# A decoder layer on one core: GpSimd's elementwise work in the router stage moved to VectorE and ScalarE, rank products a tile later

## The chip, the cores and the metric

One core of one Trainium2 chip runs the kernel. Its engines are TensorE (PE in the profile, with PEld for the loads of the stationary operand), VectorE (DVE), ScalarE (ACT), GpSimd (POOL) and SyncE (SP, which issues most DMAs). The metric is the device time of one execution in microseconds (us).

## The reference, cut to what matters

One decoder layer over 512 tokens of width 1024, all in float32. After two attention branches, a gated sum goes through `w_out`; the result is normalised, and a router picks one of four groups and two of its eight experts for every token:

```python
mixed = sigmoid(g_sb) * (o_sb @ w_sb) + sigmoid(g_mla) * (o_mla @ w_mla)
x  = layer_norm(ALPHA * x + gate1 * (mixed @ w_out), ln1_g, ln1_b)
u2 = x * (1 + scale2) + shift2
g_idx   = top_1(softmax(u2 @ w_rg + b_rg))                 # of 4 groups
top_idx = top_2((u2 @ w_re + b_re) of that group)          # of 8 experts
moe = sum over the two experts of weight * (silu(u2 @ w_g) * (u2 @ w_u)) @ w_d
x  = layer_norm(ALPHA * x + gate2 * moe, ln2_g, ln2_b)
```

## The kernel before, in words

**Order of the work.** The program is traced once and a planner orders each engine's queue by its own estimate of times, with program order as the priority; each engine then executes its queue strictly in order. Inside a `manual_schedule` block the named engines keep the order in which the block was written; two such blocks can still be interleaved with one another.

**The stages around the change.** (1) Both attentions run until about 397 us. (2) The MLA branch product: for each of eight blocks m of 128 columns, PE multiplies the branch weights (split into a high and a low part, `whi` by ScalarE L681, `wlo` by VectorE L682) with the attention output, three matmuls for each of four k. `evac_mix` then gates the result (L717, VectorE), adds the other branch's part (L718, GpSimd), casts to `mixh` (L719, ScalarE) and subtracts to `mixl` (L722, VectorE). (3) The product with `w_out`, again three matmuls for each of eight k, tile t of 128 tokens and column half nh. `split_wo(nh, kh)` makes the high and low parts of four k: it multiplies the loaded rows by `gate1` (L799, GpSimd and VectorE in turn), casts (L800, ScalarE) and subtracts (L801, VectorE). The split (1, 1) writes the buffer `RB`, which (0, 1) held. The half nh = 0 runs for all four tiles at once into four PSUM banks `o`; `evac_o` adds the residual x (L810) and takes statistics (L811), both on VectorE. In the middle of that half the norm's gain and bias are loaded into `lng1` and scaled by ALPHA (L887, GpSimd).

(4) **The tile loop.** The half nh = 1 runs tile by tile into PSUM banks `oh` (two buffers). Between its matmuls the loop places the routing of the tile before: `route_half` transposes the unnormalised row block (L971), copies it (`vT`, L973 VectorE and L974 ScalarE) and multiplies it by the router weights (`pl`, L976); `norm1` turns the statistics into scale and shift; `norm1_out` writes the normalised rows to the DRAM tensor `xhd` (cast L941 on ScalarE, DMA from GpSimd's queue L943), and for tiles 0 and 1 also the affine result (two GpSimd operations over 128x1024, L947) to `xnd` (L948). `route` is a chain of small VectorE operations from the logits (L980) by two maxima with their indices and a cast (L989) to the one-hot rows `A` (L991) and their sum `Ab` (L992), followed at once by the **rank products** on PE (L994), which count for each token how many tokens before it chose the same expert.

(5) After the loop, a chain of small VectorE operations goes from the counts (L1023, L1027) to the gather indices `gidx` (L1055). Other short chains are traced behind it: the table of expert slots (L1071 to L1092), the softmax weights (`combine_weights`, L1146 to L1154), the overflow list (L1174 to L1177). (6) GpSimd's queue gathers rows of `xhd` by `gidx` (L1133), which are transposed (L954), made affine (L960, L958) and fed to the experts.

**Weights of the experts.** They come in pieces of 1 MB into a ring of 15 buffers, each of which is a buffer of the earlier stages first (`W1` held `lng1`, `B0` and `B1` the rows x); SP issues a load as soon as the buffer is free, in the order of its queue.

Of the kernel before, what the change touches and what calls it, by code (L numbers as in the profile page):

```python
# [17 lines left out]
ALU = mybir.AluOpType  # L18
# [34 lines left out]
def tile_layer(ctx: ExitStack, tc: tile.TileContext, x, c, positions, w_ada, b_ada, w_in, mla_q_norm_g, w_q_up,  # L53
# [661 lines left out]
    def evac_mix(a, m):  # L715
        g0, g1 = part(gat, m), part(gat, 8 + m)
        DVE.tensor_tensor(g1, a, g1, ALU.mult)  # L717
        POOL.tensor_tensor(g0, g0, g1, ALU.add)  # L718
        ACT.copy(part(mixh, m), g0)  # L719
        for n in range(2):  # L720
            lo = slice(n * 2 * P, (n + 1) * 2 * P)
            DVE.tensor_tensor(mixl[n][:, m, :], g0[:, lo], part(mixh, m)[:, lo].bitcast(F32), ALU.subtract)  # L722
# [67 lines left out]
    def split_wo(nh, kh):  # L790
        t = raws["wo", nh, kh]
        tags = wtag[nh, kh]
        if len(tags) == 1:
            w8 = gran(tags[0], [KD, 512], F32R, "wo")
            hi, lo = w8[:, 0:4, :], w8[:, 4:8, :]
        else:
            hi, lo = (gran(g, [4, 512], F32R, "wo") for g in tags)
        for k in range(4):
            (POOL if k % 2 else DVE).tensor_tensor(t[:, k, :], t[:, k, :], gate1[:, nh * 512:(nh + 1) * 512], ALU.mult)  # L799
            ACT.copy(hi[:, k, :], t[:, k, :])  # L800
            DVE.tensor_tensor(lo[:, k, :], t[:, k, :], hi[:, k, :].bitcast(F32), ALU.subtract)  # L801
        wo[nh, kh] = (hi, lo)
# [5 lines left out]
    def evac_o(a, t, nh):  # L808
        xs = xr[t // 2][:, t % 2, nh * 512:(nh + 1) * 512]
        DVE.scalar_tensor_tensor(xs, xs, ALPHA, a, ALU.mult, ALU.add)  # L810
        DVE.bn_stats(stats[t][:, nh, :], xs)  # L811
# [66 lines left out]
    for k in range(KD):  # L878
        if k == 4:
            split_wo(1, 0)  # L880
            lng1 = gran("W1", [2, D], F32, "lng1")
            load_wo(1, 1)()
            for i in range(2, 6):
                load_gran(i)
            for n, v in enumerate((ln1_g, ln1_b)):
                SP.dma_start(lng1[:, n], v[0].partition_broadcast(P))
            POOL.tensor_scalar(lng1, lng1, ALPHA, None, ALU.mult)  # L887
            router_consts()
        for t in range(NT):
            mm_o(a4[t], t, k, 0, k == 0, k == KD - 1)  # L890
# [46 lines left out]
    def norm1_out(t):  # L937
# [6 lines left out]
        if t < 2:  # L944
            ACT.activation(r, r, AF.Identity, bias=m[:, 3:4], scale=m[:, 2:3])
            for n, op in ((0, ALU.mult), (1, ALU.add)):
                POOL.tensor_tensor(r, r, lng1[:, n], op)  # L947
            POOL.dma_start(xnd[t * P:(t + 1) * P, :], r)  # L948
# [29 lines left out]
    def route(t):  # L978
# [13 lines left out]
        DVE.tensor_tensor(Ab[:, t, :], A[:, t, 0, :], A[:, t, 1, :], ALU.add)  # L992
        for t2 in range(t + 1):
            PE.matmul(prk[:, t * 32:t * 32 + 32], triu if t2 == t else onesb, Ab[:, t2, :], start=(t2 == 0), stop=(t2 == t))  # L994

    for t in range(NT):
        a = pt("fil", 2, "oh")
        for k in range(KD):
            mm_o(a, t, k, 1, k == 0, k == KD - 1)
            if k == 1 and t > 0:  # L1000
# [3 lines left out]
            if k == 4:  # L1004
                route_half(t, 0)
        evac_o(a, t, 1)
# [9 lines left out]
    with tc.manual_schedule(engines={mybir.EngineType.Pool}):  # L1016
        norm1_out(NT - 1)
        POOL.memset(gran_tile(13)[0:1, 0:1], 0.0)
    route(NT - 1)
    for i in range(10, 14):  # L1020
        load_gran(i)
    for t in range(NT):
        PE.matmul(prk[:, 128:160], onesb, Ab[:, t, :], start=(t == 0), stop=(t == NT - 1))  # L1023

    with tc.manual_schedule(engines={mybir.EngineType.DVE}):
# [29 lines left out]
        DVE.tensor_tensor(gidx, gif[:, 0, :], gif[:, 1, :], ALU.add)  # L1055
# [14 lines left out]
    with tc.manual_schedule(engines={mybir.EngineType.DVE}):  # L1070
# [95 lines left out]
    DVE.tensor_scalar(pq[:, 0:1], pcol, -2.0, float(CAP - 1), ALU.mult, ALU.add)  # L1166
    DVE.memset(pq[:, 1:2], 1.0)
# [164 lines left out]
    with tc.manual_schedule(engines=MS):  # L1332
        start = tc.manual_schedule(engines={mybir.EngineType.DVE, mybir.EngineType.Activation})
        start.__enter__()
        combine_weights()
# [45 lines left out]
        for n, u in enumerate(units):  # L1381
# [42 lines left out]
            if n == 1:  # L1424
                y_rows()
                overflow_list()
# [229 lines left out]
```

## Time and profile before

| | |
|---|---|
| median of three runs | 825.21 us (820.85 to 825.68) |
| the profiled execution | 827.33 us, of which the span from the first to the last instruction is 825.6 us |
| PE busy | 691.5 us (84%) |
| VectorE busy | 524.3 us (64%) |
| ScalarE busy | 249.7 us (30%) |
| GpSimd busy | 217.8 us (26%) |
| mean granted clock of PE | 0.929 of 2.4 GHz |
| moved by DMA | 195.15 MB |

A busy share is a mean over stages of different kinds; the stage of the change lies between about 397 and 525 us of the span. Clock 1.00 is 2.4 GHz, and 0.50 is 1.2 GHz; a value between is a mean over a stretch with both.

### The profile page before, as it was taken

The page shows a single profiled execution, that of the slowest core. Times are in us where ns is not written, and L with a number is a line of the kernel's source. Part 1 is how long each engine was busy: PE and PEld are TensorE (multiplying, and loading weights), DVE is VectorE, ACT ScalarE, POOL GpSimd, SP SyncE. Part 2 cuts the span into 40 slices and gives each one's busy share as a digit, 9 for nine tenths or more (in the row PEclk, how much of TensorE's full clock was granted, in tenths as well). Part 3 has the DMA queues.
Part 4 walks back from the last instruction along what each step waited for, and adds up shares of the span by engine and source line. Part 5 has one row for each costly group of instructions (what it writes and reads, how often), then busy time and mean ns, then how long its engine had stood idle before and what let it go on. Part 6 is the DMA issues. An engine that isn't in the chain of part 4 may idle for free. (4 is left out here: it accounts for less than half of the span.)

```text
span 825.6 us, 10607 instructions
## 1 busy us (share of the span) xinstructions
PE 691.5 (84%) x3201; PEld 426.7 (52%) x3201; DVE 524.3 (64%) x1083; ACT 249.7 (30%) x545; POOL 217.8 (26%) x269
## 2 busy tenths in 40 slices
PE   5789999999999798999989665777889779977880
PEld 3568877677776464666668553432333223322330
DVE  3995366867746857876596766664834715543297
ACT  2123244333435434443231324342201101111411
POOL 5546022322333312200363440300000000028174
PEclk9999999999999898999999867698999889999995
DMA  9964365547612793331549348788999998899942
GB/s 266 257 178 129 111 223 197 191 153 249 207 32 66 272 363 120 89 124 54 202 180 359 124 144 286 247 292 293 389 410 417 400 415 325 298 357 402 349 183 102
DMA packets 92109, 195.15 MB, mean 236 GB/s; under 512 B 11421, under 2 KB 53498, under 8 KB 86154
## 3 DMA queue, kind: packets, MB, share of 16 engines
q1 hardware_dynamic: 88544, 182.71, 62.5%
q0 software_dynamic: 3424, 11.57, 4.0%
q8 instruction: 36, 0.59, 0.3%
q14 instruction: 31, 0.25, 0.1%
q10 hardware_dynamic: 74, 0.03, 0.0%
HBM read 173.30 MB, written 35.67 MB: 253 GB/s over the span
## 5 line engine op out<-in xcount | busy, mean ns | idle before, releaser
L1224 PE MATMUL pgu<-ex,xT 128*64 128x512 f32 (+1 forms) x608 | 119.5, 615 | 17.7 <-DMA ex<-in_w_exp_up_dram 10.6
L1224 PEld LDWEIGHTS pgu<-ex,xT 128*64 128x64 f32 (+1 forms) x608 | 49.1, 129 | 82.3 <-issue 71.1
L330 PE MATMUL acc<-uh,whi 128*128 128x512 f32 x224 | 90.9, 406 | 0.0
L330 PE MATMUL acc<-uh,wlo 128*128 128x512 f32 x224 | 88.3, 394 | 0.4 <-DVE wlo L321 0.4
L330 PE MATMUL acc<-ul,whi 128*128 128x512 f32 x224 | 87.6, 391 | 0.0
L1254 PE MATMUL py<-ex,hT 128*64 128x512 f32 (+1 forms) x304 | 66.2, 668 | 17.7 <-DVE hT L1247 12.8
L577 POOL TENSOR_TENSOR w<-be,sc 128x128 f32<-128x128 f32 (+3 forms) x32 | 39.6, 1239 | 135.6 <-DVE sc L575 113.0
L1232 ACT ACTIVATE sl<-pgu 128x256 f32<-128x256 f32 x33 | 11.4, 383 | 173.7 <-PE pgu L1224 154.3
L1294 POOL DMA_DIRECT2D lraw<-in_ln_g_dram x4 | 2.0, 510 | 203.2 <-DVE lraw L1291 203.2
L330 PEld LDWEIGHTS acc<-uh,whi 128*128 128x128 f32 x224 | 42.1, 188 | 14.6 <-issue 4.4
L321 DVE TENSOR_TENSOR wlo<-raw,whi 128x1024 fp32r<-128x1024 f32 x27 | 34.4, 1272 | 21.8 <-ACT whi L320 21.6
L330 PEld LDWEIGHTS acc<-uh,wlo 128*128 128x128 f32 x224 | 42.0, 188 | 11.2 <-DVE wlo L321 2.0
L1254 PEld LDWEIGHTS py<-ex,hT 128*64 128x64 f32 (+1 forms) x304 | 16.9, 135 | 59.2 <-issue 29.2
L443 DVE SCALAR_TENSOR_TENSOR macc<-ra,rtx,macc 128x1024 f32<-128x1024 f32 x28 | 38.4, 1394 | 13.5 <-DMA ra<-in_w_ada_dram 13.4
L330 PEld LDWEIGHTS acc<-ul,whi 128*128 128x128 f32 x224 | 42.2, 188 | 7.9 <-issue 0.2
L1233 DVE TENSOR_TENSOR sl<-pgu,sl 128x256 f32<-128x256 f32 x33 | 12.9, 419 | 43.3 <-ACT sl L1232 43.3
L320 ACT CAST whi<-raw 128x1024 fp32r<-128x1024 f32 x27 | 28.4, 1051 | 29.5 <-PE acc L330 14.2
L1247 DVE COPY hT<-phT 128x256 f32<-128x256 f32 x33 | 13.2, 419 | 32.6 <-PE phT L1239 19.7
L575 DVE TENSOR_TENSOR_SCAN sc<-al 128x127 f32<-128x127 f32 (+3 forms) x32 | 27.1, 849 | 10.5 <-ACT al L571 8.6
L817 PE MATMUL oh<-wo,mixh 128*128 128x512 f32 x64 | 28.7, 497 | 5.8 <-DVE wo L801 5.8
L536 PE MATMUL px<-ident,w 128*128 128x128 f32 x160 | 28.9, 280 | 5.3 <-POOL w L577 2.1
L1217 DVE COPY xT<-XRA 128x128 f32 (+1 forms) x30 | 7.6, 252 | 34.7 <-PE pgu L1224 29.7
(491 smaller groups left out, 1515.5 us busy)
## 6 DMA issues: line engine op xcount, KB each, us to landing
ex<-in_w_exp_gate_dram SPq DMA_DIRECT2D x64, 512.0 KB
ex<-in_w_exp_up_dram SPq DMA_DIRECT2D x64, 512.0 KB
ex<-in_w_exp_down_dram SPq DMA_DIRECT2D x32, 1024.0 KB
ra<-in_w_ada_dram SPq DMA_DIRECT2D x16, 1024.0 KB
raw<-in_w_in_dram SPq DMA_DIRECT2D x12, 1024.0 KB
Ys<-dq SPq DMA_DIRECT2D x10, 1024.0 KB
ada<-in_w_ada_dram SPq DMA_DIRECT2D x16, 512.0 KB
rwo<-in_w_out_dram SPq DMA_DIRECT2D x6, 1024.0 KB
```

What stands on the lines that cost most here:

```text
L320: ACT.copy(hi, w)
L321: DVE.tensor_tensor(lo, w, hi.bitcast(F32), ALU.subtract)
L330: PE.matmul(a, w_[:, k, :], part(u_, k), start=(k == 0 and n == 0), stop=(k == nk - 1 and n == 2))
L443: DVE.scalar_tensor_tensor(o, v, cact[:, k, 0:1], o, ALU.mult, ALU.add)
L536: PE.transpose(px[:, kt * P:(kt + 1) * P], w[:, kt * P:(kt + 1) * P], ident)
L575: DVE.tensor_tensor_scan(sc[:, 0:W - 1][:, ::-1], al[:, 1:W][:, ::-1], al[:, 1:W][:, ::-1], 1.0, ALU.mult, ALU.bypass)
L577: POOL.tensor_tensor(w[:, 0:W], be[:, 0:W], sc[:, 0:W], ALU.mult)
L817: PE.matmul(a, u_, w_[:, k % 4, :], start=first and n == 0, stop=last and n == 2)
L1224: PE.matmul(ps_t[rows, :], xT[u, t][:, k, rows], ew[e, k // 4][:, :, k % 4, :], start=(k == 0), stop=(k == KD - 1))
L1233: DVE.tensor_tensor(sl, ps_t[:, DE:2 * DE], sl, ALU.mult)
L1247: DVE.tensor_copy(hT[u, min(t, 1)][:, t // 2], phT[:, o:o + 256].rearrange("p (k n) -> p k n", k=2))
L1254: PE.matmul(pys[nh][rows, :], hT[u, min(t, 1)][:, t // 2, k, rows], ew[e, 2][:, k, nh * 512:(nh + 1) * 512], start=(k == 0), stop=(k == 1))
```

## The change

`evac_mix`: the add goes to VectorE. `split_wo`: no multiply by `gate1` for the first column half, all four on VectorE for the second; instead `evac_o` multiplies the first half's PSUM result in place. `lng1` is scaled on ScalarE. The affine of tiles 0 and 1 leaves `norm1_out`, goes to VectorE and is called two tiles later, as are the rank products; the products of the counts are issued for three tiles before the last tile's routing. The first four k of tiles 0 and 1 of the second half run ahead of the loop. The short chains that aren't part of the way to `gidx` are queued behind it on VectorE.

```diff
@@ evac_mix
         DVE.tensor_tensor(g1, a, g1, ALU.mult)
-        POOL.tensor_tensor(g0, g0, g1, ALU.add)
+        DVE.tensor_tensor(g0, g0, g1, ALU.add)
         ACT.copy(part(mixh, m), g0)
@@ split_wo
         for k in range(4):
-            (POOL if k % 2 else DVE).tensor_tensor(t[:, k, :], t[:, k, :], gate1[:, nh * 512:(nh + 1) * 512], ALU.mult)
+            if nh:
+                DVE.tensor_tensor(t[:, k, :], t[:, k, :], gate1[:, 512:1024], ALU.mult)
             ACT.copy(hi[:, k, :], t[:, k, :])
@@ evac_o
+        if nh == 0:
+            DVE.tensor_tensor(a, a, gate1[:, 0:512], ALU.mult)
         DVE.scalar_tensor_tensor(xs, xs, ALPHA, a, ALU.mult, ALU.add)
@@ first half, k == 4
-            POOL.tensor_scalar(lng1, lng1, ALPHA, None, ALU.mult)
+            ACT.activation(lng1, lng1, AF.Copy, scale=ALPHA)
@@ norm1_out
         if t < 2:
             ACT.activation(r, r, AF.Identity, bias=m[:, 3:4], scale=m[:, 2:3])
-            for n, op in ((0, ALU.mult), (1, ALU.add)):
-                POOL.tensor_tensor(r, r, lng1[:, n], op)
-            POOL.dma_start(xnd[t * P:(t + 1) * P, :], r)
+
+    def norm1_affine(t):
+        r = xr[t // 2][:, t % 2, :]
+        for n, op in ((0, ALU.mult), (1, ALU.add)):
+            DVE.tensor_tensor(r, r, lng1[:, n], op)
+        POOL.dma_start(xnd[t * P:(t + 1) * P, :], r)
@@ route and the tile loop
         DVE.tensor_tensor(Ab[:, t, :], A[:, t, 0, :], A[:, t, 1, :], ALU.add)
+
+    def rank(t):
         for t2 in range(t + 1):
             PE.matmul(prk[:, t * 32:t * 32 + 32], triu if t2 == t else onesb, Ab[:, t2, :], start=(t2 == 0), stop=(t2 == t))
+    ah = {t: pt("fil", 2, "oh") for t in range(2)}
+    for t in range(2):
+        for k in range(4):
+            mm_o(ah[t], t, k, 1, k == 0, False)
     for t in range(NT):
-        a = pt("fil", 2, "oh")
-        for k in range(KD):
+        a = ah[t] if t < 2 else pt("fil", 2, "oh")
+        for k in range(4 if t < 2 else 0, KD):
             mm_o(a, t, k, 1, k == 0, k == KD - 1)
-            if k == 1 and t > 0:
+            if k == (5 if t < 2 else 1) and t > 0:
                 route_half(t - 1, 1)
                 norm1_out(t - 1)
                 route(t - 1)
             if k == 4:
                 route_half(t, 0)
+            if k == 5 and t > 1:
+                rank(t - 2)
+                norm1_affine(t - 2)
@@ after the loop
+    def count(*ts):
+        for t in ts:
+            PE.matmul(prk[:, 128:160], onesb, Ab[:, t, :], start=(t == 0), stop=(t == NT - 1))
+
+    rank(NT - 2)
+    count(0, 1, 2)
     route(NT - 1)
     for i in range(10, 14):
         load_gran(i)
-    for t in range(NT):
-        PE.matmul(prk[:, 128:160], onesb, Ab[:, t, :], start=(t == 0), stop=(t == NT - 1))
+    count(3)
+    rank(NT - 1)
@@ the index chain and what follows it
-        DVE.tensor_tensor(gidx, gif[:, 0, :], gif[:, 1, :], ALU.add)
+        gidx_at = DVE.tensor_tensor(gidx, gif[:, 0, :], gif[:, 1, :], ALU.add).ins
-    with tc.manual_schedule(engines={mybir.EngineType.DVE}):
+    with tc.issue_after(gidx_at), tc.manual_schedule(engines={mybir.EngineType.DVE}):
...
+    with tc.issue_after(gidx_at):
+        DVE.tensor_scalar(pq[:, 0:1], pcol, -2.0, float(CAP - 1), ALU.mult, ALU.add)
+        DVE.memset(pq[:, 1:2], 1.0)
...
-        combine_weights()
+        with tc.issue_after(gidx_at):
+            combine_weights()
...
-                overflow_list()
+                with tc.issue_after(gidx_at):
+                    overflow_list()
```

`issue_after(i)` queues what its block traces on the engine of instruction `i` behind `i`.

## Rows read from the trace of the kernel before

**Rows 1.** The page, part 1 (busy us of an engine, share of the span, instructions) and one group of part 5 (line, engine, operation, output and inputs, count, busy us and mean ns of one, idle time before).

```profile
PE 691.5 (84%) x3201; PEld 426.7 (52%) x3201; DVE 524.3 (64%) x1083; ACT 249.7 (30%) x545; POOL 217.8 (26%) x269
...
L321 DVE TENSOR_TENSOR wlo<-raw,whi 128x1024 fp32r<-128x1024 f32 x27 | 34.4, 1272 | 21.8 <-ACT whi L320 21.6
```

**Rows 2.** The table by stage: from and to in us, length, then busy us and instructions of PE, PEld, VectorE, ScalarE and GpSimd, the granted clock, the DMA engines' share and GB/s.

```profile
397.00:417.00 20.00, 17.41 (x72) 12.47 (x71) 13.80 (x29) 6.32 (x11) 8.20 (x6) 1.00 0.58 196
417.00:430.00 13.00, 9.95 (x35) 7.23 (x35) 13.00 (x15) 4.14 (x7) 9.20 (x6) 0.87 0.24 85
430.00:450.00 20.00, 20.00 (x106) 17.16 (x105) 12.20 (x14) 4.57 (x8) 8.53 (x6) 1.00 0.90 341
450.00:462.00 12.00, 6.20 (x26) 4.67 (x25) 12.00 (x17) 2.18 (x4) 5.58 (x2) 0.86 0.55 220
462.00:475.00 13.00, 12.22 (x61) 9.93 (x61) 7.00 (x22) 6.09 (x7) 3.38 (x3) 0.86 0.36 121
475.00:490.00 15.00, 10.49 (x47) 8.38 (x47) 10.59 (x23) 4.49 (x5) 6.93 (x5) 0.75 0.38 141
490.00:505.00 15.00, 12.82 (x63) 9.95 (x62) 7.89 (x27) 3.30 (x4) 2.71 (x5) 0.79 0.64 200
505.00:515.00 10.00, 1.44 (x14) 1.17 (x13) 8.41 (x54) 5.98 (x8) 0.61 (x2) 0.58 0.98 367
```

**Rows 3.** PE's waits between 397 and 515 us: who waited for what, us in total, times, longest.

```profile
PE prk L994 <- DVE Ab L992: 10.0, 3, 3.4
PE oh L817 <- DVE wo L801: 5.8, 1, 5.8
...
PE o L817 <- DVE wo L801: 1.6, 1, 1.6
PE o L817 <- ACT wo L800: 1.4, 1, 1.4
```

**Rows 4.** PE in order of time: start us, us, engine, line, operation, output and input, shape, count of merged instructions.

```profile
430.15 0.62 PE L817 MATMUL o<-wo,mixh 128*128 128x512 f32 x2
...
430.84 0.62 PE L817 MATMUL o<-wo,mixh 128*128 128x512 f32 x2
...
461.74 1.05 PE L817 MATMUL oh<-wo,mixh 128*128 128x512 f32 x2
...
463.02 1.05 PE L817 MATMUL oh<-wo,mixh 128*128 128x512 f32 x2
...
467.19 0.60 PE L971 MATMUL pu<-ident,xr_B 128*128 128x128 f32 x4
...
467.86 0.39 PE L817 MATMUL oh<-wo,mixl_R 128*128 128x512 f32 x1
...
468.32 0.62 PE L976 MATMUL pl<-rtx,vT 128*128 128x40 f32 x4
...
469.10 0.39 PE L817 MATMUL oh<-wo,mixl_R 128*128 128x512 f32 x1
```

**Rows 5.** VectorE in order of time, the tile loop.

```profile
457.26 4.78 DVE L801 TENSOR_TENSOR wo<-rwo,wo 128x512 fp32r<-128x512 f32 x4
...
472.81 1.93 DVE L989 CAST ixf<-ix 128x2 f32<-128x2 uint32 x1
474.78 2.54 DVE L991 TENSOR_SCALAR A<-iot,ixf 128x32 f32<-128x32 f32 x2
...
498.63 0.26 DVE L980 SCALAR_TENSOR_TENSOR Lg<-pl,mv,msk_mla 128x40 f32<-128x40 f32 x1 [0.90 <-PE pl L976]
...
500.81 0.16 DVE L989 CAST ixf<-ix 128x2 f32<-128x2 uint32 x1
501.01 0.39 DVE L991 TENSOR_SCALAR A<-iot,ixf 128x32 f32<-128x32 f32 x2
```

**Rows 6.** GpSimd in order of time, the same stretch.

```profile
456.05 5.37 POOL L887 TENSOR_SCALAR lng<-lng 128x2048 f32<-128x2048 f32 x1 [5.84 <-DMA lng<-in_ln_b_dram]
...
472.35 4.79 POOL L947 TENSOR_TENSOR xr_B<-xr_B,lng 128x1024 f32<-128x1024 f32 x2 [0.29 <-DVE Lg L986]
```

**Rows 7.** Three lines of the kernel: count, then min/median/max ns of one, first and last start in us.

```profile
L717 DVE TENSOR_TENSOR gat<-acc,gat x8: 677/682/691, 398.7 to 426.5; 128x512 f32<-128x512 f32 x8
...
L718 POOL TENSOR_TENSOR gat<-gat,gat x8: 1295/1666/1670, 399.4 to 427.2; 128x512 f32<-128x512 f32 x8
...
L817 PE MATMUL oh<-wo,mixh x64: 388/476/797, 450.3 to 503.2; 128*128 128x512 f32 x64
```

**Rows 8.** VectorE in order of time, behind the tile loop: the count, the gather indices and the first affine of gathered rows.

```profile
510.48 0.19 DVE L1027 COPY cnt<-prk 128x32 f32<-128x32 f32 x1
...
516.64 0.16 DVE L1055 TENSOR_TENSOR gidx<-gif 128x8 int32<-128x8 f32 x1
...
522.85 1.37 DVE L960 TENSOR_SCALAR XRA<-pxg,vc 128x128 f32<-128x128 f32 x4 [3.95 <-PE pxg L954]
```

**Rows 9.** GpSimd in order of time: issues of the first and third gather.

```profile
517.09 1.12 POOL L1133 DMA_INDIRECT xg<-xhd,gidx  x1 [7.42 <-DVE gate L1175]
...
519.83 0.99 POOL L1133 DMA_INDIRECT xg<-xhd,gidx  x1 [0.30 <-issue]
```

**Rows 10.** SP's waits between 395 and 520 us, in the same form as rows 3.

```profile
SPq L865 <- POOL xr_B L947: 15.9, 1, 15.9
```

**Rows 11.** The table by stage for a stretch of the expert stage, in the form of rows 2.

```profile
600.00:620.00 20.00, 18.02 (x84) 7.25 (x86) 5.12 (x11) 0.77 (x2) 0.00 (x0) 1.00 1.02 414
```

More of the change, by code (lines that the diff above doesn't have):

```diff
@@ L1165, in tile_layer @@
     pq = posf[:, 0, :]
-    DVE.tensor_scalar(pq[:, 0:1], pcol, -2.0, float(CAP - 1), ALU.mult, ALU.add)
-    DVE.memset(pq[:, 1:2], 1.0)
+    with tc.issue_after(gidx_at):
+        DVE.tensor_scalar(pq[:, 0:1], pcol, -2.0, float(CAP - 1), ALU.mult, ALU.add)
+        DVE.memset(pq[:, 1:2], 1.0)
     ovt = gate1[:, 0:5 * 32 * TOV].rearrange("p (a e k) -> p a e k", a=5, e=32)
```

## The prediction

> **What bounds the kernel now.** I read the page first: PE is busy for 84% of the span [rows 1]. Busy time doesn't say at which clock, so the second view is the table by stage [rows 2]. Before 397 us nothing is edited, and from 525 us on the expert stage runs. Between them lies the router stage, and there PE is neither idle for good nor full: from 450 to 505 us it is busy 41.7 of 55 us at a granted clock of 0.75 to 0.86, while from 430 to 450 us it is busy all the time at 1.00. The third view is PE's own waits [rows 3]: three waits of about 3.4 us for `Ab` (L992) in front of the rank products (L994), two of them in the tile loop and one at its end; 5.8 us for the second split of `w_out` (L801); 1.6 and 1.4 us for its first split. None of these is a wait for a transfer. The fourth view is PE in order of time [rows 4]: three matmuls of 512 columns follow one another in 0.69 us at 2.4 GHz (430.15 to 430.84), and in 1.28 us right behind the stall that ended at 460.3 (461.74 to 463.02), which is the level of 1.2 GHz. So every stall is paid twice: once as idle time, once as slow matmuls after it.
>
> Why VectorE is late is in its rows beside GpSimd's [rows 5, 6]. In the first tile the two compares of L991 (128x32) take 2.54 us and the cast before them 1.93; in the third tile the same take 0.39 and 0.16. The slow pair lies inside GpSimd's two 128x1024 operations of L947 (472.35 to 477.1), the fast one beside nothing on GpSimd. The four subtractions of L801 take 4.78 us from 457.26, while GpSimd scales `lng1` (456.05 to 461.4). So what bounds the stage is one chain, PE to VectorE to PE, whose VectorE part is stretched by GpSimd's elementwise work.
>
> **The change part by part.**
>
> *MLA product loop, `evac_mix` (397 to 420 us).* Eight adds leave GpSimd, 1.67 us each, and become VectorE adds; the nearest row is the multiply of the same shape in front of them, 0.68 [rows 7]. ScalarE's cast to `mixh` waits for that add, and the cast for a later weight split stands behind it in ScalarE's queue, so the add is on PE's loop. PE idles 2.6 us in 397 to 417 [rows 2]. VectorE gets 8 x 0.68 = 5.4 us in a stage where it is busy 13.8 of 20. I take back 2.0 of the 2.6 us; bounds 0.6 and 2.6.
>
> *First split of `w_out` (417 to 430 us).* The first half loses its multiplies (four on VectorE, four on GpSimd), so ScalarE casts straight from the loaded rows. PE's waits of 1.4 and 1.6 us go, and the matmuls at the slow clock after them, some 3.7 us at 1.28 instead of 0.69 per three, cost 3.7 x (1 - 0.69/1.28) = 1.7 us. Together 4.7 us; I take 4.4, lower bound 2. The loads of the next rows, which start when a `raw` buffer is free, come earlier too.
>
> *First gate in PSUM.* `evac_o` gets four multiplies of 128x512 from PSUM; 0.68 each by the row of L717 [rows 7], 2.7 us, on VectorE between the two column halves. They delay the second split L801 behind them, because that split writes the buffer which the first half has just finished reading. Twelve evacuation operations of about 0.65 us are 7.8 us, begun some 1.4 us before the first half ends; the first L801 is then ready 7 us after that end. PE now has both first tiles' first four k to run, 24 matmuls x 0.23 = 5.5 us, where it had 12. A wait of about 1.5 us is left of 5.8.
>
> *`lng1` scaled on ScalarE.* 2048 columns once. Hidden: ScalarE is busy 2.2 of 12 us in 450 to 462 [rows 2]. If its queue puts it ahead of the casts of the second split and the load is late, those casts and PE wait with it, up to the 5.4 us that the same step took on GpSimd [rows 6].
>
> *The tile loop (450.3 to 503.7 us, 53.4 us [rows 7]).* Rank products move to a tile later: they no longer stand in PE's queue in front of the next matmuls, so the two stalls of 3.4 us go, with or without GpSimd. The affine of tiles 0 and 1 goes to VectorE, four operations of 128x1024; the nearest row of two SBUF inputs, L321, has 1.27 [rows 1], 5.1 us. I count both engines again from the end of the first half. PE: 96 matmuls x 0.23 = 21.8; seven half tiles of transposes and logits, which add 0.44 (467.19 to 467.86 less one matmul) and 0.55 (468.32 to 469.10 less one) [rows 4], are 6.9; ranks 0.7; the wait above 1.5: 31 us. VectorE: 7.8 + 4 x 0.65 for L801 = 10.4; for each of three tiles 1.4 for the two halves of the residual step, 1.0 for the small norm steps, 0.8 for copies and 3.0 for the routing chain (498.63 to 501.6 [rows 5]), 18.6; affine 5.1; less the 1.4 us that it starts earlier: 32.7 us. Two queues that are both nearly full and wait for one another do not reach the larger of the sums; I add 3 us. That makes 35.5, a gain of 17.9. Bounds: PE alone without that wait, 29.5 (gain 23.9), and with the waits of the first rival below some 47 (gain 7).
>
> *The chain after the loop (503.7 to 516.8 us).* From the count (510.48) to the gather indices (516.64) VectorE takes 6.3 us [rows 8], and works on other chains between the steps of this one. The eighteen steps' own durations and their hand-overs sum to about 5.4 us; the rest, 0.9, comes back when the others stand behind `gidx`, and the earlier count products give 0.1: gain 1.0, bounds 0 and 1.5.
>
> *What now stands behind `gidx`.* Some 25 small operations of the slot table and the softmax weights, about 5 us on VectorE, then the first affine of gathered rows. Before, that affine began 6 us after `gidx` (522.85), waiting for the gathers. So they just fit, and cost 0 to 2 us. Here a rule speaks against the change. The rows show the first gather's issue on GpSimd taking 1.12 us beside busy VectorE and 0.99 later [rows 9]: 0.13 us for each, nothing. The Trainium skill, "SBUF — State Buffer", section "Who interferes with whom", states that descriptor generation on GpSimd waits while VectorE runs an operation in a mode that takes both SBUF ports; the block moved behind `gidx` would then hold up every gather. The 0.13 us of this trace do not bear that out for operations as small as these.
>
> *Weight prefetch.* The load of a buffer that `lng1` held waits 15.9 us on SP's queue for L947 [rows 10], with later weight loads behind it. Now it waits for the VectorE affine of tile 1, near the end of the loop, and four loads of 1 MB start almost together there, beside the gathers. The DMA engines are 98% busy in 505 to 515 already [rows 2]; I take 1.0 us on the first gathers, bounds 0 and 3. GpSimd's queue too now waits for that affine, to issue the store `xnd`; behind it stands the last tile's store `xhd`, which is ready only some 5 us after the loop, so nothing is lost there. In the expert stage the DMA engines are full (600 to 620 us, 414 GB/s [rows 11]), but each of its loads is started by PE releasing a buffer, so the stage shifts as a whole.
>
> Sum: 2.0 + 4.4 + 17.9 + 1.0 - 1.0 = 24.3 us. The profiled execution took 827.33 us with a span of 825.6, the median is 825.21; I take the gain from the median: **801 us**.
>
> **The rivals.** *VectorE becomes the bound.* For: the sums of 31 and 32.7 are as good as equal, and VectorE does its queue in order, so an affine of 2.5 us can stand ahead of the copy that PE's logits need. Against: PE's prefetch of 24 matmuls and ranks that nobody waits for. Price: a stall of 2.5 us in each of three tiles and some 2.2 us of slow clock after each, 14 us less the 3 taken: the gain falls to 13, **812 us**.
>
> *The gathers or the weights give it back.* VectorE's block behind `gidx` holds the gathers up for its 5 us, or the four late loads delay them and the first experts' weights by as much. For: the full DMA engines of 505 to 515 us. Against: the 0.13 us of [rows 9]. The gain falls to about 19, **806 us**. (By the rule of the Trainium skill, "SBUF — State Buffer", named above, the time would end here.)
>
> *Slower: the slow VectorE rows are not GpSimd's doing.* Then VectorE takes over 5.4 + 2.7 + 5.1 = 13.2 us and gets none of its slow rows back, on the path that bounds the stage: **838 us**. It decides if L801 and L991 stay above 1 us with GpSimd empty. Against it stands that the slow rows begin and end with GpSimd's in both tiles that have L947, and the tiles without it have none.
>
> *The planner undoes it*: where the rank products or the late operations end up is decided by its own estimate of times. One of the loop's three rank products met no wait even in the old order [rows 3]; with GpSimd empty the others would cost some 1 us each instead of 3.4: 803 us, inside the forecast.
>
> **How the numbers follow.** Forecast 0.66 (with the planner's case), VectorE bound 0.20, gathers or weights 0.10, slower 0.03, the rest 0.01. The lower end is the sum of the better bounds, with the loop at PE's own 29.5 us (no wait left for the second split): 2.6 + 4.7 + 23.9 + 1.0 = 32.2 us, 793; the upper end takes in the first rival and a little of its spread, 814. A measurement of this kernel can tell some 1%, 8 us, from no change. Faster by over that: all but the slower case and the far end of the first rival, 0.93; within it 0.04; slower 0.03.
>
> **What will show it.** Rows of L991 near 0.2 us each and of L801 near 0.68 in all tiles; no L994 among PE's long waits; the granted clock near 1.00 in 420 to 470 us; the last `oh` matmul near 479 us; `gidx` 13 us or less behind it; the expert stage as long as before. Wrong would be: a new wait of PE for L973 or for the affine, the `lng1` step ahead of the casts on ScalarE, first gathers that land later than 6 us after `gidx`, or waits for weights in the first two expert units.

## The result, and the profile after

The changed kernel takes 796.34 us (median of four runs, 795.10 to 798.51), the kernel before 823.12 on the same chip: a ratio of 0.9677 (0.9633 to 0.972), 26.8 us less. In a second set of runs the ratio was 0.9654 (0.9606 to 0.9702). The prediction was 801 us, 793 to 814.

The profiled execution took 796.89 us, with a span of 795.0. Its page, part 1, which answers to [rows 1]:

```profile
PE 679.4 (85%) x3201; PEld 425.4 (54%) x3201; DVE 510.3 (64%) x1099; ACT 252.1 (32%) x546; POOL 174.5 (22%) x248
```

VectorE has 16 instructions more and is busy 14.0 us less: it has taken over work and lost more waiting than that. The table by stage, in the form of [rows 2]:

```profile
397.00:417.00 20.00, 19.75 (x87) 15.91 (x86) 19.02 (x38) 9.76 (x17) 0.00 (x0) 1.00 0.71 229
417.00:430.00 13.00, 13.00 (x75) 11.39 (x74) 6.34 (x17) 2.71 (x5) 0.00 (x0) 1.00 0.78 266
430.00:450.00 20.00, 20.00 (x97) 16.63 (x96) 17.36 (x30) 7.82 (x12) 0.00 (x0) 1.00 0.79 301
450.00:462.00 12.00, 11.79 (x73) 9.72 (x72) 8.44 (x36) 7.42 (x8) 0.81 (x1) 1.00 0.63 220
462.00:475.00 13.00, 11.76 (x74) 9.24 (x72) 10.94 (x39) 5.38 (x8) 2.73 (x6) 1.00 0.69 238
```

PE is busy nearly without a gap until the loop's end at 472.7 us, and the granted clock is 1.00 in every stretch of this table; before it was 0.75 to 0.87 in five of the seven stretches from 397 to 505 us [rows 2]. PE's waits between 397 and 478 us, all of them (before: [rows 3]):

```profile
PE pu L977 <- DVE xr_B L813: 0.7, 1, 0.7
PE pl L982 <- DVE vT L979: 0.5, 1, 0.5
PE acc L330 <- DVE gat L717: 0.2, 1, 0.2
PE pl L982 <- ACT vT L980: 0.2, 1, 0.2
```

The first two come behind the loop's end, at 473.5 and 474.6 us; inside the tile loop PE waits 0.2 us. Behind the loop one wait for `Ab` is left (3.2 us).

VectorE in order of time, the routing of the first two tiles (L995, L997 and L953 are the cast, the compares and the affine; the first two were L989 and L991 in [rows 5]):

```profile
460.31 0.15 DVE L995 CAST ixf<-ix 128x2 f32<-128x2 uint32 x1
460.50 0.38 DVE L997 TENSOR_SCALAR A<-iot,ixf 128x32 f32<-128x32 f32 x2
461.03 1.22 DVE L953 TENSOR_TENSOR xr_B<-xr_B,lng 128x1024 f32<-128x1024 f32 x1
464.58 0.16 DVE L995 CAST ixf<-ix 128x2 f32<-128x2 uint32 x1
465.79 0.38 DVE L997 TENSOR_SCALAR A<-iot,ixf 128x32 f32<-128x32 f32 x2
```

With GpSimd empty the first tile's cast takes 0.15 us instead of 1.93 and its compares 0.38 instead of 2.54.

**Where the time went.** The start of the stage wanders by up to 3.6 us from one profiled execution to the next (396.5 to 400.1), so I count from it: from the start of the first gate multiply of `evac_mix` (L717) to the end of PE's last matmul of the product loop, of the first half (`o`) and of the second (`oh`), to the end of `gidx`, to the start of the first gather and to the first `gate_up` matmul of the experts. Each is one row of the order of time. All profiled executions, in us from the stage's start, with the ratio of the runs:

| kernel | product loop | o | oh | gidx | gather | gate_up | ratio |
|---|---|---|---|---|---|---|---|
| before | 21.2 | 51.8 | 105.0 | 118.1 | 118.4 | 128.2 | 1 |
| after | 17.5 | 42.9 | 75.3 | 87.8 | 89.8 | 99.7 | 0.9677 (0.9633 to 0.972) |
| after_again | 17.5 | 42.9 | 75.3 | 87.8 | 90.2 | 100.4 | 0.9654 (0.9606 to 0.9702) |
| moves_only | 17.5 | 42.9 | 74.5 | 87.8 | 88.6 | 98.1 | 0.9647 (0.9615 to 0.9678) |
| order_only | 21.2 | 50.2 | 100.2 | 112.6 | 113.3 | 122.9 | 0.9896 (0.9871 to 0.9921) |
| affine_pool | 17.5 | 42.9 | 82.4 | 94.7 | 95.0 | 106.9 | 0.9727 (0.9696 to 0.9759) |
| dummy_pool | 17.5 | 42.9 | 85.9 | 99.4 | 99.7 | 109.4 | 0.9734 (0.9696 to 0.9772) |
| mix_add_pool | 21.2 | 46.6 | 81.0 | 93.3 | 94.5 | 104.4 | 0.9679 (0.9647 to 0.9711) |
| lng_pool | 17.5 | 42.9 | 80.9 | 93.5 | 95.7 | 105.3 | 0.9693 (0.9652 to 0.9735) |
| gate_in_split | 17.5 | 44.0 | 79.4 | 91.8 | 95.1 | 104.6 | 0.9705 (0.9675 to 0.9734) |
| split_pool | 17.5 | 47.3 | 81.7 | 94.3 | 97.0 | 106.6 | 0.9747 (0.9704 to 0.979) |
| no_issue_after | 17.5 | 42.9 | 75.3 | 88.6 | 89.3 | 99.2 | 0.9638 (0.9602 to 0.9674) |
| weights_later | 17.5 | 42.9 | 75.7 | 88.3 | 88.6 | 98.1 | 0.9667 (0.9637 to 0.9698) |
| moves_chain_later | 17.5 | 42.8 | 74.5 | 87.0 | 87.3 | 97.0 | 0.9655 (0.961 to 0.97) |

From before to after: product loop 3.7, first half 5.3 (30.6 to 25.4), tile loop 20.7 (53.2 to 32.4), chain to `gidx` 0.7, less 1.8 behind `gidx`: 28.5 us at the first `gate_up`, beside the 26.8 and, in the second set, 27.8 us between the medians. The experts behind it take as long as before, 298.0 against 298.8 us of the span; over the fourteen profiled executions this stretch is 295.1 to 300.5 us long, so a change of 2 or 3 us in it could not be told.

### The profile page after: what moved, and what is told of

Read it like the earlier page. It is cut to its first block, busy times and chain, and to the rows that moved or that the text cites. A ratio compares the mean times of both kernels' runs of the same rounds, so it can differ in the third digit from the quotient of the medians.

```text
span 795.0 us, 10593 instructions
## 1 busy us (share of the span) xinstructions
PE 679.4 (85%) x3201; PEld 425.4 (54%) x3201; DVE 510.3 (64%) x1099; ACT 252.1 (32%) x546; POOL 174.5 (22%) x248
## 5 line engine op out<-in xcount | busy, mean ns | idle before, releaser
L1247 PE MATMUL pgu<-ex,xT 128*64 128x512 f32 (+1 forms) x608 | 117.8, 612 | 13.6 <-DMA ex<-in_w_exp_up_dram 6.4
L1247 PEld LDWEIGHTS pgu<-ex,xT 128*64 128x64 f32 (+1 forms) x608 | 53.2, 129 | 73.0 <-issue 61.3
L1277 PE MATMUL py<-ex,hT 128*64 128x512 f32 (+1 forms) x304 | 68.5, 692 | 22.4 <-DVE hT L1270 13.9
L320 ACT CAST whi<-raw 128x1024 fp32r<-128x1024 f32 x27 | 28.4, 1051 | 29.5 <-PE acc L330 14.3
L1270 DVE COPY hT<-phT 128x256 f32<-128x256 f32 x33 | 13.2, 419 | 32.2 <-PE phT L1262 18.7
L536 PEld LDWEIGHTS px<-ident,w 128*128 128x128 f32 x160 | 19.9, 140 | 17.1 <-issue 3.6
```

The source lines that it names most:

```text
L320: ACT.copy(hi, w)
L536: PE.transpose(px[:, kt * P:(kt + 1) * P], w[:, kt * P:(kt + 1) * P], ident)
L1247: PE.matmul(ps_t[rows, :], xT[u, t][:, k, rows], ew[e, k // 4][:, :, k % 4, :], start=(k == 0), stop=(k == KD - 1))
L1270: DVE.tensor_copy(hT[u, min(t, 1)][:, t // 2], phT[:, o:o + 256].rearrange("p (k n) -> p k n", k=2))
L1277: PE.matmul(pys[nh][rows, :], hT[u, min(t, 1)][:, t // 2, k, rows], ew[e, 2][:, k, nh * 512:(nh + 1) * 512], start=(k == 0), stop=(k == 1))
```

## The experiments

**The moves or the order.** Theory: GpSimd's elementwise operations hold VectorE's up, and the moves are the gain. Rival: the stalls come from where the rank products stand, and the order is worth as much by itself. `moves_only` keeps every move and takes the order of the kernel before:

```diff
         DVE.tensor_tensor(Ab[:, t, :], A[:, t, 0, :], A[:, t, 1, :], ALU.add)
-
-    def rank(t):
         for t2 in range(t + 1):
...
-    ah = {t: pt("fil", 2, "oh") for t in range(2)}
...
                 norm1_out(t - 1)
+                if t < 3:
+                    norm1_affine(t - 1)
                 route(t - 1)
...
-                rank(t - 2)
-                norm1_affine(t - 2)
...
-    count(0, 1, 2)
...
-    count(3)
+    count(0, 1, 2, 3)
...
-    with tc.issue_after(gidx_at):
```

> The changed kernel with the old order: GpSimd's elementwise work is moved, but ranks follow their routing at once, no k runs ahead, the affine follows its own tile, and the chain to the gather indices is not kept free. Theory A (GpSimd holds VectorE up while it works): the slow rows of L989 and L991 are gone (0.2 and 0.4 us for the pair), the first two stages keep their gain of 10 us, and only the run-ahead (about 3 us) and two or three rank waits of 1 us are lost: 800 to 804 us. Theory B (the order of the queues makes the gain): only the first stages gain, two rank stalls of about 3.4 us with slow matmuls behind them stay, 810 to 815 us.

Measured 797.51 us (795.29 to 799.56), under the range of its theory A. PE's waits up to 478 us are three of the four of the changed kernel: 0.7, 0.5 and 0.2. In the table it is the changed kernel to within 0.8 us up to `gidx`. So the run-ahead of 24 matmuls and the later ranks are worth nothing once GpSimd is empty; in its order of time `oh` matmuls follow the first half without a gap from 441.17 us, through 446.58 to 447.86 us, when the first two L802 are made: the planner puts other matmuls there by itself. Only `issue_after` leaves a mark: from the last `oh` matmul to `gidx` 13.3 us without it, 12.5 with it.

`order_only` is the reverse: all elementwise work back on GpSimd, the gate back in the split, the new order kept.

> The changed kernel with all elementwise work back on GpSimd, and the gate back in the split: only the order is new. Theory A: the two rank stalls and a part of the wait for the second split go, but VectorE stays slow beside GpSimd and the first stages stay as they were: a gain of 8 to 14 us, 809 to 815 us. Theory B: 800 to 804 us. If the two halves add up, the gain here and that of the run with the moves alone sum to 27 us; if they do the same thing twice, to more.

Measured 819.08 us (818.36 to 821.49): less gain than expected. Against the 827.60 us of the kernel before on the same chip the order gains 8.5 us and the moves 30.1, together far more than the whole change: both work on the same stalls. The two waits for `Ab` in the loop are gone, and another has come. PE's waits from 449 to 500 us:

```profile
PE pl L979 <- DVE vT L976: 5.7, 1, 5.7
PE oh L817 <- DVE wo L801: 5.0, 2, 3.9
```

and what stood ahead of that copy (`vT`, L976), VectorE and GpSimd in order of time:

```profile
476.91 4.83 POOL L950 TENSOR_TENSOR xr_B<-xr_B,lng 128x1024 f32<-128x1024 f32 x2 [0.29 <-DVE vT L976]
477.06 2.27 DVE L989 TENSOR_TENSOR Lg<-Lg,ixf 128x32 f32<-128x32 f32 x1
479.47 2.32 DVE L935 SCALAR_TENSOR_TENSOR msk_mla<-rtx,mv 128x40 f32<-128x40 f32 x1
483.19 4.78 POOL L950 TENSOR_TENSOR xr_B<-xr_B,lng 128x1024 f32<-128x1024 f32 x2
483.29 2.31 DVE L989 TENSOR_TENSOR Lg<-Lg,ixf 128x32 f32<-128x32 f32 x1
485.75 0.41 DVE L976 COPY vT<-pu 128x256 f32<-128x256 f32 x1
```

Three small operations of 2.3 us each stand in VectorE's queue ahead of a copy for the logits. With GpSimd's work still in place, putting the rank products later moved the stall to the next consumer of VectorE's work.

**Is it GpSimd at all, and without any wait for it?** `affine_pool` is the changed kernel with the affine of two tiles on GpSimd (L953, `DVE` to `POOL`). `dummy_pool` leaves the affine on VectorE and adds two GpSimd products of 128x1024 for each of tiles 0 and 1, whose result nobody reads:

```diff
         POOL.dma_start(xhd[t * P:(t + 1) * P, :], v)
         if t < 2:
+            for n in range(2):
+                POOL.tensor_tensor(rings["w"][0].rearrange("p a n -> p (a n)"), v, lng1[:, n], ALU.mult)
```

> The changed kernel with only the affine of tiles 0 and 1 back on GpSimd, two tiles late as changed. Nothing on PE waits for it. Theory A: VectorE's routing rows beside it take 1.5 to 2.5 us again, PE's logits wait for the copies behind them, and the tile loop is 2 to 5 us longer, 798 to 801 us. Theory B: VectorE is 5 us shorter of work and the loop the same or up to 2 us shorter, 794 to 796 us.

> The changed kernel with four additional products of 128x1024 on GpSimd, behind the stores of the normalised rows of tiles 0 and 1, whose results nobody reads. Theory A: the VectorE rows that fall beside them become 1 to 2.4 us long, though no engine waits for GpSimd, and the loop is 3 to 8 us longer, 799 to 804 us. Theory B: no row changes and the time stays within 1 us of 796.

Measured 804.19 us (802.12 to 806.23) and 805.22 (802.58 to 808.04), both above the range of theory A: the tile loop is 7.1 and 10.6 us longer, where 2 to 5 and 3 to 8 were expected. PE's longest wait is the one for the logits copy, in `affine_pool` (first line) and in `dummy_pool`:

```profile
PE pl L982 <- DVE vT L979: 4.7, 1, 4.7
PE pl L984 <- DVE vT L981: 4.9, 2, 2.8
```

The granted clock over the tile loop is 0.91 and 0.90 in them, 1.00 in the changed kernel. `affine_pool`, VectorE and GpSimd in order of time:

```profile
459.26 2.38 POOL L953 TENSOR_TENSOR xr_B<-xr_B,lng 128x1024 f32<-128x1024 f32 x1 [0.37 <-ACT xr_B L948]
459.46 2.21 DVE L995 CAST ixf<-ix 128x2 f32<-128x2 uint32 x1
461.71 3.03 DVE L997 TENSOR_SCALAR A<-iot,ixf 128x32 f32<-128x32 f32 x2
462.33 2.36 POOL L953 TENSOR_TENSOR xr_B<-xr_B,lng 128x1024 f32<-128x1024 f32 x1
465.86 0.17 DVE L995 CAST ixf<-ix 128x2 f32<-128x2 uint32 x1
466.07 0.39 DVE L997 TENSOR_SCALAR A<-iot,ixf 128x32 f32<-128x32 f32 x2
```

`dummy_pool`, the same view:

```profile
460.68 2.41 POOL L949 TENSOR_TENSOR w<-xh,lng 128x1024 f32<-128x1024 f32 x1
460.80 0.17 DVE L989 MAX8 gm<-Lg 128x8 f32<-128x8 f32 x1
460.98 0.18 DVE L996 FIND_INDEX8 ix<-em,Lg 128x8 uint32<-128x32 f32 x1
461.21 1.91 DVE L997 CAST ixf<-ix 128x2 f32<-128x2 uint32 x1
463.69 3.87 DVE L955 TENSOR_TENSOR xr_B<-xr_B,lng 128x1024 f32<-128x1024 f32 x1
464.09 2.38 POOL L949 TENSOR_TENSOR w<-xh,lng 128x1024 f32<-128x1024 f32 x1
468.02 1.20 DVE L955 TENSOR_TENSOR xr_B<-xr_B,lng 128x1024 f32<-128x1024 f32 x1
```

The cast that started at 461.21 ended at 463.12; GpSimd's product, begun at 460.68, ended at 463.09. In `affine_pool` the cast ends at 461.67 and the product at 461.64. Both kernels have the slow rows beside GpSimd's and none where GpSimd is empty, and in `dummy_pool` PE, VectorE and ScalarE wait nowhere for GpSimd's result. That settles the rival that the slow VectorE rows are not GpSimd's doing. Four products that nobody needs put the last `oh` matmul 10.6 us later.

**What each move is worth.** One move undone at a time. `mix_add_pool`: the add of `evac_mix` on GpSimd (L718, `DVE` to `POOL`).

> The changed kernel with one edit undone: the eight adds of evac_mix are on GpSimd again. Theory (GpSimd's elementwise operations block VectorE's): the product loop ends about 3.7 us later (418 to 419 instead of 414.7), since PE waits for the gate multiply of VectorE (0.7 us each) in four of the eight blocks as in the kernel before; the rest shifts as a whole: 800 us, ratio about 0.972. Rival (my prediction's sum, in which only PE's idle time inside 397 to 417 us comes back): 2.0 to 2.6 us. Rival that the loop's gain came from elsewhere, for instance an earlier start: under 1 us.

The product loop is 21.2 us long, to a tenth that of before: the add alone is its whole 3.7 us, and the tile loop loses 2.0 more (34.4 against 32.4). The measured medians (800.14 against 797.99 and 797.26 of two neighbours on the same chip) show 2 to 3 us of these 5.7, less than the runs can tell apart; the ratio of 0.9679 is below the 0.972 expected. Why it costs so much, in order of time:

```profile
409.15 0.68 DVE L717 TENSOR_TENSOR gat<-acc,gat 128x512 f32<-128x512 f32 x1
409.91 1.67 POOL L718 TENSOR_TENSOR gat<-gat,gat 128x512 f32<-128x512 f32 x1 [2.53 <-DVE gat L717]
411.61 0.62 ACT L719 CAST mixh<-gat 128x512 fp32r<-128x512 f32 x1 [3.05 <-POOL gat L718]
412.26 0.76 DVE L722 TENSOR_TENSOR mixl_R<-gat,mixh 128x256 fp32r<-128x256 f32 x2 [1.83 <-ACT mixh L719]
412.94 0.68 DVE L717 TENSOR_TENSOR gat<-acc,gat 128x512 f32<-128x512 f32 x1
413.77 0.47 PE L330 MATMUL acc<-dkvo,whi 128*128 128x512 f32 x1 [0.75 <-DVE gat L717]
```

Here it is no blocked operation: L717 and the subtractions L682 take 0.68 us each, as without GpSimd. VectorE stands idle 1.83 us in front of L722, which waits for the add's result through ScalarE; the next block's L717, whose bank PE waits for, stands behind it in the same queue.

`lng_pool`: `lng1` scaled on GpSimd (L890).

> The changed kernel, but lng1 is scaled on GpSimd again (one operation of 128x2048, 5.4 us in the kernel before). Theory (a GpSimd elementwise operation holds VectorE's up for its length): it runs once the loads of lng1 have landed, some 4 to 5 us behind the end of the first column half, beside the residual steps and the second split; VectorE's operations there take 1.2 to 5 us instead of 0.65 each, and the loop from the end of the first half to the last oh matmul, 32.4 us in the changed kernel, becomes 35 to 38 us. Total 799 to 802, ratio 0.970 to 0.975. Rival (the 24 matmuls run ahead cover it): under 1 us, ratio as the changed kernel's.

Measured 799.71 us (796.14 to 803.49); the tile loop becomes 38.1 us instead of 32.4, at the upper end of what was expected. In order of time:

```profile
448.57 5.37 POOL L890 TENSOR_SCALAR lng<-lng 128x2048 f32<-128x2048 f32 x1 [57.67 <-DVE stats L814]
449.00 4.35 DVE L802 TENSOR_TENSOR wo<-rwo,wo 128x512 fp32r<-128x512 f32 x2
453.28 1.28 DVE L800 TENSOR_TENSOR rwo<-rwo,gate 128x512 f32<-128x512 f32 x2
```

PE then waits 3.3 us for L802 in spite of the 24 matmuls run ahead.

`gate_in_split`: the multiply by `gate1` in `split_wo` for both halves, all on VectorE, and none in `evac_o`. `split_pool`: the same with every second one on GpSimd (`POOL if k % 2 else DVE`), as before.

```diff
-            if nh:
-                DVE.tensor_tensor(t[:, k, :], t[:, k, :], gate1[:, 512:1024], ALU.mult)
+            DVE.tensor_tensor(t[:, k, :], t[:, k, :], gate1[:, nh * 512:(nh + 1) * 512], ALU.mult)
...
-        if nh == 0:
-            DVE.tensor_tensor(a, a, gate1[:, 0:512], ALU.mult)
```

> The changed kernel with the first gate multiply back in split_wo for both column halves, all eight multiplies on VectorE, and none in evac_o. Theory (the first split's gain came from GpSimd's multiplies leaving, and the gate in PSUM adds only what VectorE hides): VectorE does the first split's four multiplies of 0.68 us ahead of ScalarE's casts, so the first half starts up to 1.5 us later, the second half sees the same or an earlier second split: total within 0 to 3 us above the changed kernel, ratio 0.968 to 0.972. Rival (the gate in PSUM is what shortens the first half): the first half starts and ends 4 to 5 us later, ratio 0.973 to 0.975. Rival (its four multiplies between the halves cost more than they bring): 1 to 2 us faster than the changed kernel.

> The changed kernel, but split_wo and evac_o are those of the kernel before: four multiplies of each half split on VectorE and four on GpSimd, in turn, and no gate in PSUM. Counted from the start of the stage (the first gate multiply of evac_mix): the product loop unchanged (17.5 us); with all multiplies on VectorE the last oh matmul came 4.1 us later than in the changed kernel (79.4 against 75.3). Theory (the multiplies cost more on GpSimd, 1.7 us each, and hold VectorE's subtractions up): 6 to 9 us later, total 802 to 805, ratio 0.973 to 0.977. Rival (the gate in the split is the cost, whichever engine does it): 3.5 to 5 us later, ratio 0.970 to 0.972.

Measured 801.62 us (798.41 to 802.38) and 802.66 (800.14 to 807.19). The first half starts at the same 17.3 us with the gate in the split as without, but it ends 1.2 us later and the tile loop grows by 2.9: VectorE has eight multiplies more in the splits and four fewer in PSUM. The next rows arrive later for it: VectorE, idle for their transfer in both kernels, begins the next split's multiplies 40.5 us from the start instead of 34.9. In the tile loop PE idles 1.6 us more, mostly for that split, and is busy 1.3 us longer at the same clock of 1.00. With half of them on GpSimd the first half starts 1.9 us later and ends 4.4 later, and `oh` ends at 81.7 instead of 79.4. So of this move's 6.4 us, 4.1 are the gate itself and 2.3 GpSimd.

One at a time, the marks of `oh` are 5.7 (add), 5.7 (`lng1`), 6.4 (split and gate) and 7.1 us (affine) later than in the changed kernel, 24.9 us together, against 29.7 from before to after.

**What happened behind gidx.** The first gather starts 2.0 us behind `gidx` in the changed kernel, 0.3 before. Two theories: it waits for the last tile's store of `xhd` to land, which the weight loads delay; or VectorE's block of small operations behind `gidx` holds it up. `weights_later` keeps that block and issues three of the four late weight loads behind the first four gathers (and leaves out a one-element memset in front of one of them); `no_issue_after` takes the block away and keeps the loads.

```diff
-        POOL.memset(gran_tile(13)[0:1, 0:1], 0.0)
...
-    for i in range(10, 14):
-        load_gran(i)
+    load_gran(12)
...
         gather(0, 7, 1, 6)
+        for i in (10, 11, 13):
+            load_after(i)
```

> The changed kernel, but of the four 1 MB weight loads that start between 467 and 479 us only one keeps its place; three (granules 10, 11 and 13 of the ring) are issued behind the first four gathers. Theory: in the changed kernel the first gather starts 2.0 us behind gidx (485.21 to 487.23), against 0.3 us before, because it waits for the landing of the last tile's store xhd (issued 478.26, up to 8.1 us to land while the weight loads fill the DMA engines). Then the store lands within some 4 us, the first gather starts 0.3 us behind gidx (about 485.5), and the first gate_up follows 1.5 to 2 us earlier (about 495.3 instead of 497.1). The total, if the expert stage shifts as a whole: 1.5 to 2 us under the changed kernel, ratio to the kernel before about 0.966. Rival: the gather waits for the block of small VectorE operations behind gidx; then its start stays 2.0 us behind gidx, and the total does not move. Second rival: the first part holds but the three late loads make PE wait for weights later by as much or more; then the total is the same or up to 8 us worse, and the waits stand on loads of w_exp.

> The changed kernel without the queueing of the short chains behind gidx. Theory: gidx comes 0.5 to 1.0 us later (485.7 to 486.2), the first gather still starts near 487 because the store of the last tile lands then; the total is the same within 1 us (ratio 0.967 to 0.969). Rival: the chain's order is worth its full 1.0 us at the end and more, through the slot table that no longer stands in front of the affine of gathered rows: up to 2 us either way.

The changed kernel: from the queue of GpSimd in order of time, the last store and the first gather.

```profile
478.26 0.53 POOL L946 DMA_DIRECT2D xhd<-xh  x1 [4.22 <-ACT xh L944]
487.23 1.12 POOL L1155 DMA_INDIRECT xg<-xhd,gidx  x1 [8.36 <-DVE sc L1102]
```

The time to landing of that store alone, and the stage table's row for the time it is under way:

```profile
DMA to landing us min/median/max: 8.1/8.1/8.1
```

```profile
480.00:485.00 5.00, 0.36 (x8) 0.37 (x8) 4.17 (x15) 0.00 (x0) 0.00 (x0) 0.50 1.01 404
```

`weights_later`, the same three views:

```profile
479.61 0.53 POOL L946 DMA_DIRECT2D xhd<-xh  x1 [4.20 <-ACT xh L944]
486.86 1.13 POOL L1153 DMA_INDIRECT xg<-xhd,gidx  x1 [6.71 <-DVE sc L1092]
```

```profile
DMA to landing us min/median/max: 4.0/4.0/4.0
```

```profile
480.00:485.00 5.00, 0.29 (x5) 0.18 (x4) 4.17 (x15) 0.62 (x1) 0.14 (x1) 0.50 0.37 151
```

With the DMA engines 37% busy instead of full the store lands in 4.0 us instead of 8.1, and the gather starts 0.3 us behind `gidx` (done at 486.57) with the block in place. The profile puts the gather's wait down to a small VectorE operation in both kernels; with the same operations in place the wait is gone, so it was the landing. Without the block, `no_issue_after`, `gidx` is done 0.8 us later and the gather starts 0.7 us behind it, when the store (7.5 us) has landed. One rule fits all fourteen profiled executions: the first gather starts 0.3 us behind `gidx` or 0.9 behind the landing of the last store, whichever is later. In the totals, `weights_later` 797.99 us (795.78 to 799.98) and `no_issue_after` 797.26 (791.65 to 799.05), a gain of 1.5 us could not be seen: runs of the changed kernel lie between 790.78 and 799.28.

**A version from what was found.** `moves_chain_later`: the moves, `issue_after` and the late loads; ranks at once, no run-ahead. Beside it the changed kernel again.

> A version that takes from the change only what the runs so far found of use: the moves off GpSimd, and the chain to gidx kept free of other operations; ranks at once, no matmuls run ahead, affine right behind its own tile; and three of the four late 1 MB weight loads issued behind the first four gathers. From the start of the stage: last oh matmul 74.5 us, gidx done about 87.2 (12.5 to 12.7 behind it), first gather 0.3 us later, first gate_up about 97 (changed kernel: 99.7). If the expert stage shifts as a whole: 2 to 2.5 us under the changed kernel, ratio about 0.965. Rival: the expert stage, whose DMA engines are full, gives it back in waits for weights: no difference to the changed kernel.

> The changed kernel itself, on the same chip as the three others, so that they are compared with it directly: ratio 0.968, within 0.963 to 0.972; the marks from the start of the stage (product loop 17.5, first half's end 42.9, last oh matmul 75.3, gidx done 87.8, first gather 89.8, first gate_up 99.7) the same within 0.2 us up to gidx, and the first gather 1 to 2 us behind it.

The marks came as expected: `gate_up` at 97.0 us against 100.4. The totals can't tell: 796.08 us (790.76 to 798.88) and 797.44 (790.78 to 799.28), ratios of 0.9655 and 0.9654. In the profiled executions the 3.4 us are gone at the end: from the first `gate_up` to the end of the span it is 300.5 us against 295.8. The second rival of `weights_later`, that PE then waits longer for weights, is not what the rows show. PE's waits for the experts' weights behind that mark, the largest line in `moves_chain_later` and in `after_again`:

```profile
PE pgu L1235 <- DMA ex<-in_w_exp_up_dram: 5.6, 4, 3.6
PE pgu L1247 <- DMA ex<-in_w_exp_up_dram: 5.3, 4, 2.5
```

With the smaller lines it is 6.8 us against 6.2, and 7.0 in `after`. Between 480 and 490 us the DMA engines move 90 GB/s against 368, but over the first 120 us of the stage 267 against 260: what was put off has been made up by then. As the stretch behind the mark varies by 5.4 us over all profiled executions, what takes the 3.4 us stays open; no version here beats the changed kernel by more than can be measured.

## Why the prediction was right, and where its steps were not

**The bound and its cause: right from the first split on.** VectorE was stretched by GpSimd, and the stalls were paid twice. The rows of L991 and L801 are as short as forecast, no rank product is among PE's waits in the loop, the clock is 1.00 there, and `dummy_pool` shows the cause by itself. In the product loop it was another: no row was stretched and the clock was 1.00 before, too.

**Product loop: 3.7 us, predicted 2.0, and above its upper bound of 2.6.** The path was another than predicted: not the cast for a later split in ScalarE's queue, but L722 in VectorE's, with L717 behind it (`mix_add_pool`). And I took the gain for PE's idle time. PE's busy time fell as well: between the loop's start and end it is 18.59 us for 75 recorded matmuls before and 17.26 us for 76 after, at clock 1.00 both times. Matmuls that don't wait start 0.23 us apart, though each record is 0.39 us long; at a wait this overlap is lost. In `mix_add_pool` the matmul at 413.77 starts 1.14 us after the one before it, 0.91 more than 0.23, for 0.75 us of idle time, and itself takes 0.47 us. Idle time is no upper bound for what a stall costs, even without a change of clock.

**First split and first half: 5.3 us, predicted 4.4, bound 4.7.** The argument holds. PE idled 3.1 us in this half before and not at all after, as costed; its busy time fell by 2.2 us (27.56 to 25.36, granted clock 0.94 and 1.00), where 1.7 was costed for the slow matmuls. The gate in PSUM, which I costed only as a delay of the second split, has a gain of its own (`gate_in_split`, 4.1 us at the last `oh` matmul): it replaces eight multiplies by four, and the next rows come earlier, as the prediction said without a price.

**Second split: no wait left, predicted 1.5 of 5.8.** `oh` matmuls fill the 6 us until the first L802 is done, in `moves_only` too.

**Tile loop: 20.7 us, predicted 17.9; the reason given for the ranks was wrong, and so was the bound.** "so the two stalls of 3.4 us go, with or without GpSimd": `order_only` refutes it. Without GpSimd's work they go whichever way the ranks are ordered; with it they come back as a logits wait of 5.7 us. The loop before and after, in the form of [rows 2]:

```profile
450.46:503.62 53.16, 40.59 (x190) 32.14 (x188) 35.72 (x83) 16.06 (x20) 17.83 (x10) 0.81 0.47 166
440.26:472.68 32.42, 32.21 (x186) 26.33 (x184) 26.46 (x80) 17.80 (x21) 2.44 (x4) 1.00 0.63 218
```

PE's idle time falls by 12.4 us and its busy time by 8.4, with the clock up from 0.81 to 1.00: the stalls paid twice. PE is idle 0.2 us, so the 3 us added for two queues that wait for one another do not show. PE's own work, costed at 29.5 us, takes 32.2; VectorE's, costed at 32.7, takes 26.5. VectorE did not become the bound, PE did. That the term came within 2.8 us is in part luck: VectorE's sum and the 3 us were too much, and PE's work was too little. (The sum has two slips of 0.2 to 0.3 us: 96 x 0.23 is 22.1, and 32.7 and 3 are 35.7.)

**Chain 1.0: measured 0.7 to 0.8, and given back.** The term behind it, −1.0 (0 to 3), was −1.8: I named the four weight loads beside the gathers, but not the step they act on. The store of the last tile was counted as "ready only some 5 us after the loop, so nothing is lost there"; its landing is what set the gather. One sign of being wrong that the prediction named did come: the first gather landed 6.6 us behind `gidx`, and the first affine of gathered rows began 7.8 us behind it instead of 6.0.

**The rule on descriptor generation.** Gather issues take 1.12 us and then 0.99 to 1.01 in the changed kernel beside the block, as in [rows 9], and `weights_later` shows no delay with the block in place. The rule of the Trainium skill, "SBUF — State Buffer", section "Who interferes with whom", did not decide the time here; beside VectorE operations longer than these it was not tried.

The steps that were too small (1.7, 0.9 and 2.8 us), less the 1.1 us by which the chain and what stands behind it fell short, are 4.2 us after rounding, the distance between the 24.3 us of the sum and the 28.5 us of the marks. The 801 us also started from a median of 825.21 us over three runs; over four it is 823.12, which is 2.1 of the 4.7 us between 801 and 796.34.

## What to carry to other kernels

When small operations of one engine are ten times as long in one tile as in the next, look for a second engine's row that spans them, and cure that before reordering the consumers: the reorder alone moves the stall to the next consumer in the queue. Cost a stall by the marks of a stage, not by its idle time alone. A transfer that is started earlier meets others: look at what has to land before the next step, not only at the next step's own issue.

## What the runs showed of the hardware

Which VectorE operations GpSimd holds up follows their operands. Beside a GpSimd elementwise operation, `TENSOR_TENSOR` with both inputs in SBUF (128x32: 2.27 to 2.31 us instead of 0.19), `CAST` of 128x2 (1.91 to 2.21 in the rows shown, instead of 0.16) and `TENSOR_SCALAR` are held; `MAX8` and `FIND_INDEX8` (0.17, 0.18) and the copy from PSUM (0.41, inside GpSimd's 483.19 to 487.97 in `order_only`) are not. The Trainium skill, "SBUF — State Buffer", section "Who interferes with whom", states just this split: two SBUF inputs against a GpSimd operation that reads SBUF, and copies, casts and `tensor_scalar` in their two-port modes, are locked out for the whole instruction, others not. The rows agree, with one difference. Beside the scaling of `lng1` (`TENSOR_SCALAR` of 128x2048 on GpSimd) only the first subtraction is held, and it ends 1.2 us before GpSimd's operation: at 460.23 of 461.42 us before, at 452.76 of 453.94 in `lng_pool`. The next ones take 0.68 us beside its rest.

A store of 512 KB from GpSimd's queue landed in 3.1 us in `moves_chain_later` and 4.0 in `weights_later`, with the DMA engines 60 and 56% busy while it was under way, and in 8.1 and 8.5 us in `after` and `after_again`, with the engines full; the first gather started 0.9 us behind that landing in the last two.
